# Four more stages of a decoder layer with the two parts of the activation side by side in one 512-column product

## The chip, the cores and the metric

The kernel runs on one core of one Trainium2 chip. Its engines are TensorE (PE in the profile, its weight loads PEld), VectorE (DVE), ScalarE (ACT), GpSimd (POOL) and SyncE (SP); each works through its own instructions in order. The metric is the device time of one run in microseconds, the median of the runs shown.

## The reference, cut to what matters

One layer over 256 tokens of width 1024, in float32: two self-attention mixers, cross-attention to 256 memory tokens, and a gated feed-forward block of width 2816.

```python
x = x + concat(rms(moba(h)), subln(diff(h))) @ w_out        # h = rms(x) * g, projected by w_in
h2, m = rms_norm(x, norm_g), rms_norm(mem, mem_g)
q, k, v = h2 @ wq, m @ wk, m @ wv                           # 4 heads of 256
o = softmax(q @ k.T / 16) @ v
x = x + o @ wo
h3 = rms_norm(x, ffn_norm_g)
x = x + (silu(h3 @ w_gate) * (h3 @ w_up)) @ w_down
out = rms_norm(x, final_norm_g)
```

## The kernel before

Every big product is done with numbers that are split in two: a is H + L, where H is a copy in the reduced type fp32r and L = a - H. Of the four partial products three are kept: wH aH, wH aL and wL aH. Activations lie transposed, as eight k-tiles of 128 rows by 256 tokens. Weights come in 65 chunks of 1 MB by DMA (`wr`); each chunk is split in four parts by `wpart`, ScalarE making `wh` (L124) and VectorE `wl` (L109).

A projection takes one chunk of 256 output rows: eight steps, one for each k-tile, and in a step two output halves c. There are two ways to do a step. `ws` (L302) does three products of 256 columns for each c, into one PSUM tile of 128x2x256 that holds both halves:

```python
for q, (m, b) in enumerate(((h, aH), (h, aL), (l, aH))):
    nc.tensor.matmul(o[:, c, :], m[:, k, cs], b[:, k, :], ...)
```

`ws2` (L310, L311) has H and L side by side in one tile (`hs`), and does one product of 512 columns with wh and one of 256 with wl for each c. It needs a PSUM tile of 512 columns for each half, and the two column halves have to be added afterwards: `add_halves` copies the right half to SBUF on ScalarE (L894) and adds the left one on VectorE (L896). The value weights (`as_`, L321) and the down projection have the weights as the moving side and are not touched here.

PSUM has eight tiles: three tagged `acc`, three `att` (attention logits and transposes), two `ob`. The order on every engine is the order in which the Python code writes instructions (a manual schedule). A count of steps, `state["slot"]`, rises by one in `tick()` after every step; `later(n, fn)` has `fn` written n steps ahead, and `tick` adds half a `wpart` for each step. So attention work, transposes and scalings are sprinkled between the steps of the projections by tables of step numbers.

The stages in order: q, k and v of the mixers (to about 100 us of the span); the four chunks of memory keys (`KH`, `KL`), with the end of the mixers' attention between their steps; half of the memory values; four chunks of `w_out` (evacuated by `residual`, which adds to `xT` at L746 and splits into `cH`, `cL`); four chunks of cross queries (`q_evac`); the other half of the memory values, with cross-attention (`cross_logits`, `cross_t`, `cross_pv`) between; four chunks of `w_co`; then 11 pairs of gate and up chunks and the down projection.

In the mixers, `diff_rstd` and `diff_scale` (L543 to L552) normalise the second mixer with one power on GpSimd (L265); `mix_t` (L567) transposes the result for `w_out`. In the feed-forward block the first five pairs use `ws` on the unscaled `h3`; the row factor R2 is applied in `glu` (L876 to L879, then the split at L293 and L294). Four calls of `scale_h` (L888, L287, L289) meanwhile scale `xT` by R2 and write `hs`, two k-tiles each; from pair 5 on `ws2` on `hs` is used, with `gate_evac` and `up_evac`. `x2_t` transposes `xT` back, for the end.

Of the kernel before, what the change touches and what calls it, by code (L numbers as in the profile page):

```python
# [17 lines left out]
P = 128  # L18
D = 1024
S = 256  # L20
# [17 lines left out]
def layer(ctx: ExitStack, tc: tile.TileContext, x, mem, mix_norm_g, w_in, moba_out_g, diff_lambda,  # L38
# [12 lines left out]
    def slot(i, dt=FR):  # L51
        return slots.tile([P, KT, S], dt, name=f"b{i}", tag=f"b{i}")

# [275 lines left out]
    hH, hL = slot(1), slot(2)  # L329
    h = (hH, hL)  # L330
    hF = slot(4, FT)
# [226 lines left out]
    def mix_t(e2):  # L558

        if "mix" not in M:  # L560
            M["mix"] = (slot(1), slot(2))
        mixH, mixL = M["mix"]
# [33 lines left out]
    m = (slot(4), slot(5))  # L596
# [104 lines left out]
    late = ctx.enter_context(tc.tile_pool(name="late", bufs=1))  # L701
# [3 lines left out]
    def cross_ops():  # L705
        return tuple(cx.tile([P, KT, S], FR, name="c" + n, tag="c" + n) for n in "HL")
# [15 lines left out]
    def pair(a, evac, by_k=False, late_kts=(6, 7)):  # L722

        w0, w1 = wuse(), wuse()
        o = [acc(), acc()]
        early = [k for k in range(KT) if k not in late_kts]
        if by_k:
            run([st for k in early for i, w in enumerate((w0, w1)) for st in ws_steps(o[i], w, a, [k])],
                done=False)
        else:  # L730
            for i, w in enumerate((w0, w1)):
                run(ws_steps(o[i], w, a, early), done=False)
        for i, w in enumerate((w0, w1)):
            run(ws_steps(o[i], w, a, late_kts))
# [34 lines left out]
    ev = residual(sqa, *h2, G_CROSS)  # L769
# [4 lines left out]
    q2 = (slot(1), slot(2))  # L774

    def q_evac(i, o):
        split(q2[0][:, 2 * i:2 * i + 2, :], q2[1][:, 2 * i:2 * i + 2, :], o)
# [50 lines left out]
    def cross_pv(hd):  # L828
        if not oT:
            oT.extend(cross_ops())  # L830
# [9 lines left out]
        split(oT[0][:, 2 * hd:2 * hd + 2, :], oT[1][:, 2 * hd:2 * hd + 2, :], o)  # L840
# [11 lines left out]
    h3 = (slot(1), slot(2))  # L852
    sqb = const.tile([P, 2, 256], FT, name="sqb")
    ev = residual(sqb, *h3, G_FFN)
    pair(oT, ev, True)
    for i in (2, 3):
        single(oT, ev, i)
# [4 lines left out]
    aHs = [slot(3), slot(4), slot(6)]  # L862
    aLs = [slot(5), slot(7), ff.tile([P, 6, S], FR, name="aL")]
# [7 lines left out]
    def glu(j, og, ou):  # L871
        R = R2[0].to_broadcast([P, 2, 256])
        t1 = ff.tile([P, 2, 256], FT, name="t1", tag="t1", bufs=2)
# [17 lines left out]
    def add_halves(o, tag):  # L891
        t = ff.tile([P, 2, 256], FT, name=tag, tag=tag, bufs=2)
        for c in range(2):
            nc.scalar.activation(t[:, c, :], o[c][:, 256:512], AF.Copy)  # L894
        for c in range(2):
            nc.vector.tensor_tensor(t[:, c, :], o[c][:, 0:256], t[:, c, :], op=OP.add)  # L896
        return t

    def gate_evac(j, o):
        t = add_halves(o, "t1")  # L900
# [4 lines left out]
    def up_evac(j, o, sg):  # L905
        t = add_halves(o, "ag")
        nc.vector.tensor_tensor(t, t, sg, op=OP.mult)
        split(*act(j), t)
# [122 lines left out]
```

## Time and profile before

| what | value |
|---|---|
| median of 3 runs | 429.34 us (429.2, 429.34, 432.31) |
| the profiled execution | 429.74 us |
| its span, first to last instruction | 428.0 us |
| mean granted TensorE clock over the span | 0.997 |
| busy: PE / PEld / DVE / ACT | 97% / 90% / 68% / 60% |
| steps of a `ws` chunk, of a `ws2` chunk | 8, 8 |

The profiled execution lies 0.40 us above the median of the runs, and 1.74 us above its own span. Busy time of PE counts pipelined products that overlap one another, so the pace of products is read from their starts and not from their durations.

### The profile page before, as it was taken

What the parts mean: (1) busy time and instruction counts of PE and PEld (TensorE: products, weight loads), DVE (VectorE), ACT (ScalarE), POOL (GpSimd) and SP (SyncE); (2) the same over time, 40 slices, a digit from 0 to 9 for tenths busy, and PEclk for the clock granted to TensorE, in tenths of its full rate; (3) what the DMA queues carried; (4) which work ended last, traced back from release to release, by engine and by line L of the source; (5) the groups of instructions that cost most, each with busy time, mean ns of one, the idle gap of its engine ahead of it and who ended that gap; (6) DMA issues with size and microseconds to landing.
All of it is one profiled execution on the core that took longest, in us unless ns stands there. A gap on an engine that the chain in (4) does not pass through costs nothing.

```text
span 428.0 us, 7419 instructions
## 1 busy us (share of the span) xinstructions
PE 417.0 (97%) x2900; PEld 386.7 (90%) x2900; DVE 290.1 (68%) x583; ACT 254.9 (60%) x550; POOL 27.5 (6%) x75
## 2 busy tenths in 40 slices
PE   8998999999999999999999999999999999999994
PEld 5996899979998999998999999999888888888883
DVE  2886738899497766586658678887666666744434
ACT  3778878789565663475546576565656655544313
POOL 4740200000010000000000100000000000000001
PEclk9999999999999999999999999999999999999998
DMA  8989782345438536344534846647763685555002
GB/s 252 302 229 278 198 238 81 118 125 190 179 115 289 187 100 195 101 129 158 192 114 121 269 151 188 186 124 242 248 196 102 194 296 186 208 197 196 1 2 98
DMA packets 57987, 74.62 MB, mean 174 GB/s; under 512 B 1688, under 2 KB 49596, under 8 KB 57952
## 3 DMA queue, kind: packets, MB, share of 16 engines
q1 hardware_dynamic: 56224, 69.87, 50.9%
q0 software_dynamic: 1424, 3.89, 4.1%
q8 instruction: 23, 0.38, 0.4%
q10 hardware_dynamic: 304, 0.40, 0.3%
q14 instruction: 12, 0.10, 0.1%
HBM read 72.50 MB, written 1.64 MB: 173 GB/s over the span
## 4 chain that ended last, share of the span: by engine, by line
PE 81%; DMA 6%; DVE 5%; POOL 3%; ACT 2%; issue 2%; POOLq 0%; DVEq 0%; ACTq 0%
PE acc L302 30%; PE y L321 13%; PE acc L321 9%; PE att L302 5%; PE acc L310 5%; PE att L310 5%; PE att L311 3%; PE acc L311 3%; DMA strip_d<-strip 2%; DMA bias<-strip_d 2%; DMA tT<-in_rel_bias_table_dram 2%; PE oc L838 1%; PE att L794 1%; DVE wl L109 1%; POOL strip L218 1%
## 5 line engine op out<-in xcount | busy, mean ns | idle before, releaser
L109 DVE TENSOR_TENSOR wl<-wr,wh 128x512 fp32r<-128x512 f32 x258 | 164.6, 684 | 32.4 <-ACT wh L124 32.0
L124 ACT ACTIVATE wh<-wr 128x512 fp32r<-128x512 f32 x258 | 146.0, 621 | 55.1 <-PE y L321 20.1
L302 PE MATMUL acc<-b,wh 128*128 128x256 f32 x688 | 128.2, 286 | 0.0
L302 PEld LDWEIGHTS acc<-b,wh 128*128 128x128 f32 x688 | 106.9, 191 | 0.3
L302 PE MATMUL acc<-b,wl 128*128 128x256 f32 x344 | 97.5, 283 | 0.5 <-DVE wl L109 0.5
L302 PEld LDWEIGHTS acc<-b,wl 128*128 128x128 f32 x344 | 65.8, 191 | 0.9 <-DVE wl L109 0.9
L321 PE MATMUL y<-wh,b 128*128 128x512 f32 (+1 forms) x190 | 51.8, 349 | 0.0
L321 PE MATMUL acc<-wh,b 128*128 128x512 f32 x128 | 40.6, 399 | 0.3 <-ACT wh L124 0.3
L321 PE MATMUL y<-wl,b 128*128 128x512 f32 (+1 forms) x110 | 38.1, 347 | 0.0
L321 PEld LDWEIGHTS y<-wh,b 128*128 128x128 f32 x190 | 33.6, 189 | 4.8
L310 PE MATMUL acc<-hs,wh 128*128 128x512 f32 x96 | 37.8, 393 | 0.0
L310 PE MATMUL att<-hs,wh 128*128 128x512 f32 x96 | 37.8, 393 | 0.0
L302 PE MATMUL acc<-cH,wh 128*128 128x256 f32 x128 | 36.4, 284 | 0.0
L302 PE MATMUL acc<-cH,wl 128*128 128x256 f32 x128 | 36.0, 281 | 0.0
L302 PE MATMUL acc<-cL,wh 128*128 128x256 f32 x128 | 36.0, 281 | 0.0
L311 PE MATMUL acc<-hs,wl 128*128 128x256 f32 x96 | 27.1, 283 | 0.0
L311 PE MATMUL att<-hs,wl 128*128 128x256 f32 x96 | 27.1, 283 | 0.0
L321 PE MATMUL acc<-wl,b 128*128 128x512 f32 x64 | 25.2, 394 | 1.5 <-DVE wl L109 1.5
L321 PEld LDWEIGHTS acc<-wh,b 128*128 128x128 f32 x128 | 22.5, 189 | 4.0 <-ACT wh L124 0.5
L302 PEld LDWEIGHTS acc<-cH,wh 128*128 128x128 f32 x128 | 24.1, 188 | 0.3 <-DVE b L294 0.2
L302 PEld LDWEIGHTS acc<-cL,wh 128*128 128x128 f32 x128 | 24.1, 188 | 0.0
L302 PEld LDWEIGHTS acc<-cH,wl 128*128 128x128 f32 x128 | 24.1, 188 | 0.0
(212 smaller groups left out, 631.2 us busy)
## 6 DMA issues: line engine op xcount, KB each, us to landing
wr<-in_w_gate_dram SPq DMA_DIRECT2D x11, 1024.0 KB, 5.5
wr<-in_w_up_dram SPq DMA_DIRECT2D x11, 1024.0 KB, 5.5
wr<-in_w_down_dram SPq DMA_DIRECT2D x11, 1024.0 KB, 4.9
wr<-in_w_in_dram SPq DMA_DIRECT2D x10, 1024.0 KB, 9.4
wr<-in_w_ck_dram SPq DMA_DIRECT2D x4, 1024.0 KB, 5.0
wr<-in_w_cv_dram SPq DMA_DIRECT2D x4, 1024.0 KB, 5.0
wr<-in_w_out_dram SPq DMA_DIRECT2D x4, 1024.0 KB, 5.0
wr<-in_w_cq_dram SPq DMA_DIRECT2D x4, 1024.0 KB, 5.0
```

Of the source, the lines that this page charges most:

```text
L109: eng.tensor_tensor(l, t, h, op=OP.subtract)
L124: nc.scalar.activation(h, t, AF.Copy)
L218: nc.gpsimd.tensor_copy(strip[:, lo:hi], tT[:, b:b + 1].to_broadcast([12, hi - lo]))
L302: nc.tensor.matmul(o[:, c, :], m[:, k, cs], b[:, k, :], start=first and c == 0 and q == 0, stop=last and q == 2, skip_group_check=True)
L310: nc.tensor.matmul(o[c], h[:, k, cs], flat(a[:, k]), start=first, stop=last, skip_group_check=True)
L311: nc.tensor.matmul(o[c][:, 0:256], l[:, k, cs], a[:, k, 0, :], start=False, stop=last, skip_group_check=True)
L321: nc.tensor.matmul(o, m[:, ka, ts], b[:, kw, cs], start=start and q == 0, stop=stop and q == 2, skip_group_check=True)
L794: nc.tensor.matmul(b[:, t, :], a[:, kt, t * P:(t + 1) * P], k[:, kt, :], start=n == 0, stop=n == 5)
L838: nc.tensor.matmul(o[:, dv, :], v[:, mt, cs], p_[:, mt, :], start=n == 0, stop=n == 5)
```

## The change

`ws2` is used where `ws` was for the four chunks of memory keys, four of `w_out`, four of cross queries, four of `w_co`, and for the gate and up chunks of pairs 2, 3 and 4: 22 chunks. The activations of these lie in tiles with H and L side by side (`both`, `hl`). `two()` takes one `acc` and one `att` tile for each chunk; `add_halves` evacuates keys and queries, and `residual` adds the four quarter tiles to `xT` one by one. The first pair of gate and up keeps `ws` (`pair1`), the second too. The four calls of `scale_h` move from steps 8, 22, 36 and 50 after the first pair to steps 6, 11, 16 and 21; a pair has 16 steps. `x2_t` moves from the second to fifth pair to the first 20 steps after the second. Names in the diff as in the kernel; line numbers in the changed kernel are higher by 7 to 32, and `add_halves` has moved up to L711 and L713.

```diff
+    def both(i, dt=FR):
+
+        return slots.tile([P, KT, 2, S], dt, name=f"b{i}", tag=f"b{i}")
+
+    def hl(t):
+        return t[:, :, 0, :], t[:, :, 1, :]
...
+    def ws2_steps(o, w, a, kts=range(KT)):
+        return [(ws2, (o, w, a, k, k == 0, k == KT - 1)) for k in kts]
...
+    def two():
+        return [flat(acc()), flat(att())]
+
+    def add_halves(o, t):
+
+        for c in range(2):
+            nc.scalar.activation(t[:, c, :], o[c][:, 256:512], AF.Copy)
+        for c in range(2):
+            nc.vector.tensor_tensor(t[:, c, :], o[c][:, 0:256], t[:, c, :], op=OP.add)
+        return t
+
     for c in range(4):
         w = wuse()
-        o = acc()
-        run(ws_steps(o, w, m))
-        split(KH[:, 2 * c:2 * c + 2, :], KL[:, 2 * c:2 * c + 2, :], o)
+        o = two()
+        run(ws2_steps(o, w, m2))
+        t = mx.tile([P, 4, 256], FT, name="bias", tag="bias", bufs=2)
+        split(KH[:, 2 * c:2 * c + 2, :], KL[:, 2 * c:2 * c + 2, :], add_halves(o, t[:, 0:2, :]))
...
     def single(a, evac, i):
         w = wuse()
-        o = acc()
-        run(ws_steps(o, w, a))
+        o = two()
+        run(ws2_steps(o, w, a))
         evac(i, o)
...
             xs = xT[:, 2 * i:2 * i + 2, :]
-            nc.vector.tensor_tensor(xs, o, xs, op=OP.add)
+            for c in range(2):
+                for cs in (slice(0, 256), slice(256, 512)):
+                    nc.vector.tensor_tensor(xs[:, c, :], o[c][:, cs], xs[:, c, :], op=OP.add)
             split_g(dH, dL, i, xs, gi)
...
     def q_evac(i, o):
-        split(q2[0][:, 2 * i:2 * i + 2, :], q2[1][:, 2 * i:2 * i + 2, :], o)
+        split(q2[0][:, 2 * i:2 * i + 2, :], q2[1][:, 2 * i:2 * i + 2, :], add_halves(o, halves_sum()))
...
-    pair(h3, lambda i, o: box.append(o))
+    pair1(hl(h3), lambda i, o: box.append(o))
     glu(0, *box)
     for i in range(4):
-        later(8 + 14 * i, scale_h, i)
-    for j in range(1, 5):
-        og, ou = acc(), att()
-        later(5, x2_t, j - 1)
-        for o in (og, ou):
-            w = wuse()
-            run(ws_steps(o, w, h3))
-        glu(j, og, ou)
-    for j in range(5, NFF // 2):
+        later(6 + 5 * i, scale_h, i)
+    og, ou = acc(), att()
+    for o in (og, ou):
+        w = wuse()
+        run(ws_steps(o, w, hl(h3)))
+    glu(1, og, ou)
+    for i in range(4):
+        later(8 + 4 * i, x2_t, i)
+    for j in range(2, NFF // 2):
         for side in range(2):
             w = wuse()
-            o = [flat(acc()), flat(att())]
-            run([(ws2, (o, w, hs, k, k == 0, k == KT - 1)) for k in range(KT)])
+            o = two()
+            run(ws2_steps(o, w, hs))
```

The first place is VectorE in the memory keys, from the second mixer transpose to the third: `b` at L576 is the transposed mixer result, `wl` the low part of weights, `b` at L294 the low part of the second key chunk, `rd`, `ssb`, `rbv` belong to `diff_rstd`, and the last two rows are `diff_scale`. Before:

```order
L576 SCALAR_TENSOR_TENSOR b_1423<-att,gT,b_1422 128x256 x2
L109 TENSOR_TENSOR wl<-wr,wh 128x512
L294 TENSOR_TENSOR b_1283<-acc,b_1282 128x512
L543 COPY rd<-rl 128x4 x2
L544 TENSOR_TENSOR ssb<-ssb,rd 128x8
L545 TENSOR_TENSOR ssb<-ssb,rd 128x8
L263 TENSOR_SCALAR rbv<-ssb 128x8
L109 TENSOR_TENSOR wl<-wr,wh 128x512 x3
L549 TENSOR_TENSOR rd<-rd,rb 128x8
L552 TENSOR_TENSOR b_1306<-oh,rd 128x512 x2
```

And in the changed kernel, where the tile of the sum is named `bias`:

```order
L585 SCALAR_TENSOR_TENSOR b_1403<-att,gT,b_1403 128x256 x2
L116 TENSOR_TENSOR wl<-wr,wh 128x512
L713 TENSOR_TENSOR bias<-acc,bias 128x256
L713 TENSOR_TENSOR bias<-att,bias 128x256
L301 TENSOR_TENSOR b_1281<-bias,b_1280 128x512
L552 COPY rd<-rl 128x4 x2
L553 TENSOR_TENSOR ssb<-ssb,rd 128x8
L554 TENSOR_TENSOR ssb<-ssb,rd 128x8
L270 TENSOR_SCALAR rbv<-ssb 128x8
L116 TENSOR_TENSOR wl<-wr,wh 128x512 x3
L558 TENSOR_TENSOR rd<-rd,rb 128x8
L561 TENSOR_TENSOR b_1301<-oh,rd 128x512 x2
```

Two additions stand ahead of the subtraction of the key chunk, and with it ahead of `diff_rstd` and `diff_scale`.

The second place is VectorE after the first pair of gate and up: the four rows from `sq` on belong to `glu`, and `z` and `hs` to `scale_h`. Before, from the end of the first `glu` to the second call of `scale_h`:

```order
L294 TENSOR_TENSOR b_2820<-ag,b_2817 128x512
L109 TENSOR_TENSOR wl<-wr,wh 128x512 x4
L888 TENSOR_TENSOR z<-xT,R_2950 128x512
L289 SCALAR_TENSOR_TENSOR hs<-z,gT,hs 128x256 x2
L109 TENSOR_TENSOR wl<-wr,wh 128x512 x5
L876 TENSOR_TENSOR t_3103<-acc,R_2950 128x512
L878 TENSOR_TENSOR sq<-sq,R_2950 128x512
L879 TENSOR_TENSOR ag<-att,sq 128x512
L294 TENSOR_TENSOR b_2820<-ag,b_2817 128x512
L109 TENSOR_TENSOR wl<-wr,wh 128x512 x2
L888 TENSOR_TENSOR z<-xT,R_2950 128x512
```

In the changed kernel, from the third call of `scale_h` to the fourth; between the end of the first `glu` and these rows lie three rows of `wl`, a call, two rows of `wl`, a call and three rows of `wl`:

```order
L918 TENSOR_TENSOR z<-xT,R_2766 128x512
L296 SCALAR_TENSOR_TENSOR hs<-z,gT,hs 128x256 x2
L116 TENSOR_TENSOR wl<-wr,wh 128x512
L906 TENSOR_TENSOR sum<-acc,R_2766 128x512
L908 TENSOR_TENSOR sq<-sq,R_2766 128x512
L909 TENSOR_TENSOR ag<-att,sq 128x512
L301 TENSOR_TENSOR b_2634<-ag,b_2635 128x2x256
L116 TENSOR_TENSOR wl<-wr,wh 128x512 x2
L918 TENSOR_TENSOR z<-xT,R_2766 128x512
L296 SCALAR_TENSOR_TENSOR hs<-z,gT,hs 128x256 x2
```

All four calls now stand on VectorE between the first `glu` and the evacuation of the third pair's gate, the last behind the second `glu`; the third pair's gate chunk reads `hs` from its first step.

## Rows read from the trace of the kernel before

**Rows 1.** The page, part 1: busy time of each engine.
```profile
PE 417.0 (97%) x2900; PEld 386.7 (90%) x2900; DVE 290.1 (68%) x583; ACT 254.9 (60%) x550; POOL 27.5 (6%) x75
```

**Rows 2.** TensorE waits: us in total, times, longest.
```profile
PE acc L321 <- DVE wl L109: 1.5, 1, 1.5
```

**Rows 3.** TensorE timeline: start us, us, engine line op out<-in; first product of four chunks.
```profile
139.36 0.40 PE L302 MATMUL acc<-b,wh 128*128 128x256 f32 x2
...
162.40 0.28 PE L302 MATMUL acc<-cH,wh 128*128 128x256 f32 x1
...
221.57 0.28 PE L302 MATMUL acc<-cH,wh 128*128 128x256 f32 x1
...
232.96 0.28 PE L302 MATMUL acc<-b,wh 128*128 128x256 f32 x1
```

**Rows 4.** Tile hs: duration min/median/max ns, first and last start us.
```profile
L310 PE MATMUL acc<-hs,wh x96: 387/396/400, 292.9 to 359.6; 128*128 128x512 f32 x96
```

**Rows 5.** Lines L894 and L896: duration min/median/max ns.
```profile
L894 ACT ACTIVATE t<-acc x6: 365/366/386, 298.4 to 355.4; 128x256 f32<-128x256 f32 x6
L896 DVE TENSOR_TENSOR t<-acc,t x6: 424/424/425, 298.8 to 355.8; 128x256 f32<-128x256 f32 x6
```

**Rows 6.** Timelines around the third mixer transpose: VectorE, GpSimd, TensorE.
```profile
119.67 0.69 DVE L294 TENSOR_TENSOR b<-acc,b 128x512 fp32r<-128x512 f32 x1
...
121.19 2.01 POOL L265 TENSOR_TENSOR rb<-rbv,mhalf 128x8 f32<-128x8 f32 x1 [13.74 <-DVE rbv L263]
...
123.44 1.29 DVE L552 TENSOR_TENSOR b<-oh,rd 128x512 f32<-128x512 f32 x2
...
124.45 0.88 PE L567 MATMUL att<-ident,b 128*128 128x128 f32 x4
```

**Rows 7.** Timelines in the cross-attention part: ScalarE, then TensorE.
```profile
183.11 0.56 ACT L805 ACTIVATE ec<-att,nmc,r1s 128x256 f32<-128x256 f32 x1
...
184.17 0.59 ACT L293 ACTIVATE b<-acc 128x512 fp32r<-128x512 f32 x1
...
183.52 0.60 PE L821 MATMUL att<-ident,ec 128*128 128x128 f32 x4
...
186.52 1.60 PE L794 MATMUL att<-b,b 128*128 128x256 f32 x12
```

**Rows 8.** VectorE timeline at the end of the cross output.
```profile
240.69 0.16 DVE L764 COPY tr<-att 128x2 f32<-128x2 f32 x1 [0.33 <-PE att L761]
```

**Rows 9.** VectorE timeline at the start of the gate and up products, and TensorE.
```profile
250.28 2.49 DVE L109 TENSOR_TENSOR wl<-wr,wh 128x512 fp32r<-128x512 f32 x4
252.69 0.68 DVE L888 TENSOR_TENSOR z<-xT,R 128x512 f32<-128x512 f32 x1
253.95 0.89 DVE L289 SCALAR_TENSOR_TENSOR hs<-z,gT,hs 128x256 fp32r<-128x256 f32 x2 [0.58 <-ACT hs L287]
254.75 3.09 DVE L109 TENSOR_TENSOR wl<-wr,wh 128x512 fp32r<-128x512 f32 x5
...
257.76 0.68 DVE L876 TENSOR_TENSOR t<-acc,R 128x512 f32<-128x512 f32 x1
...
261.93 1.29 DVE L109 TENSOR_TENSOR wl<-wr,wh 128x512 fp32r<-128x512 f32 x2
...
257.08 0.40 PE L302 MATMUL acc<-b,wh 128*128 128x256 f32 x2
```

**Rows 10.** TensorE timeline at the start.
```profile
1.22 2.74 PE L198 MATMUL clock<-still 128*128 128x512 bf16 x6 [1.22 <-DVE still L195]
...
5.03 2.82 PE L281 MATMUL xb<-ident,b 128*128 128x128 f32 x12 [0.87 <-DMA b<-in_x_dram]
7.65 1.06 PE L654 MATMUL clock<-still 128*128 128x512 bf16 x2
```

**Rows 11.** Windows at the end: us, then busy us per engine, PEclk, DMA.
```profile
420.00:422.00 2.00, 1.68 (x15) 1.47 (x13) 1.72 (x6) 1.05 (x4) 0.00 (x0) 1.00 0.67 233
...
424.00:426.00 2.00, 0.00 (x0) 0.00 (x0) 0.33 (x2) 0.27 (x1) 0.00 (x0) 0.86 0.55 194
```

More of the change, by code (lines that the diff above doesn't have):

```diff
@@ L328, in layer @@
     xT = const.tile([P, KT, S], FT, name="xT")
-    hH, hL = slot(1), slot(2)
-    h = (hH, hL)
-    hF = slot(4, FT)
+    h = hH, hL = hl(both(12))
+    hF = both(45, FT)[:, :, 0, :]
     xb = []
@@ L560, in mix_t @@
         if "mix" not in M:
-            M["mix"] = (slot(1), slot(2))
-        mixH, mixL = M["mix"]
+            M["mix"] = both(12)
+        mixH, mixL = hl(M["mix"])
         bank = att()
@@ L594, in mem_scale @@
         nc.vector.tensor_scalar(memv[:, t, :], memv[:, t, :], M["r"][:, t:t + 1], None, op0=OP.mult)
-    m = (slot(4), slot(5))
+    m2 = both(45)
+    m = hl(m2)
     def mem_t(j):
@@ L693, in layer, with halves_sum @@
     KH, KL = slot(0), slot(3)
+    def two():
[6 more added lines that the diff above has]
+        return t
     for c in range(4):
         w = wuse()
-        o = acc()
-        run(ws_steps(o, w, m))
-        split(KH[:, 2 * c:2 * c + 2, :], KL[:, 2 * c:2 * c + 2, :], o)
+        o = two()
+        run(ws2_steps(o, w, m2))
+        t = mx.tile([P, 4, 256], FT, name="bias", tag="bias", bufs=2)
+        split(KH[:, 2 * c:2 * c + 2, :], KL[:, 2 * c:2 * c + 2, :], add_halves(o, t[:, 0:2, :]))
     mixer.close()
     late = ctx.enter_context(tc.tile_pool(name="late", bufs=1))
+    def halves_sum():
+        return late.tile([P, 2, 256], FT, name="sum", tag="sum", bufs=2)
     cross = ExitStack()
@@ L705, in cross_ops @@
     def cross_ops():
-        return tuple(cx.tile([P, KT, S], FR, name="c" + n, tag="c" + n) for n in "HL")
+        return cx.tile([P, KT, 2, S], FR, name="cHL", tag="cHL")
     gfin = late.tile([P, D], FT, name="gfin")
@@ L724, in pair @@
         w0, w1 = wuse(), wuse()
-        o = [acc(), acc()]
+        o = [two(), two()]
         early = [k for k in range(KT) if k not in late_kts]
         if by_k:
-            run([st for k in early for i, w in enumerate((w0, w1)) for st in ws_steps(o[i], w, a, [k])],
+            run([st for k in early for i, w in enumerate((w0, w1)) for st in ws2_steps(o[i], w, a, [k])],
                 done=False)
@@ L731, in pair @@
             for i, w in enumerate((w0, w1)):
-                run(ws_steps(o[i], w, a, early), done=False)
+                run(ws2_steps(o[i], w, a, early), done=False)
         for i, w in enumerate((w0, w1)):
-            run(ws_steps(o[i], w, a, late_kts))
+            run(ws2_steps(o[i], w, a, late_kts))
             evac(i, o[i])
@@ L768, in layer @@
     sqa = const.tile([P, 2, 256], FT, name="sqa")
-    ev = residual(sqa, *h2, G_CROSS)
+    ev = residual(sqa, *hl(h2), G_CROSS)
     for i in range(4):
         single(M["mix"], ev, i)
-    q2 = (slot(1), slot(2))
+    q2 = hl(both(12))
     def q_evac(i, o):
-        split(q2[0][:, 2 * i:2 * i + 2, :], q2[1][:, 2 * i:2 * i + 2, :], o)
+        split(q2[0][:, 2 * i:2 * i + 2, :], q2[1][:, 2 * i:2 * i + 2, :], add_halves(o, halves_sum()))
     r1s = const.tile([P, 2], FT, name="r1s")
@@ L829, in cross_pv @@
         if not oT:
-            oT.extend(cross_ops())
+            oT.append(cross_ops())
         pH, pL = PS.pop(hd)
@@ L839, in cross_pv @@
                     n += 1
-        split(oT[0][:, 2 * hd:2 * hd + 2, :], oT[1][:, 2 * hd:2 * hd + 2, :], o)
+        H, L = hl(oT[0])
+        split(H[:, 2 * hd:2 * hd + 2, :], L[:, 2 * hd:2 * hd + 2, :], o)
     later(7, cross_rstd)
@@ L850, in layer @@
     mem_v(1)
-    h3 = (slot(1), slot(2))
+    h3 = both(12)
     sqb = const.tile([P, 2, 256], FT, name="sqb")
-    ev = residual(sqb, *h3, G_FFN)
-    pair(oT, ev, True)
+    ev = residual(sqb, *hl(h3), G_FFN)
+    pair(oT[0], ev, True)
     for i in (2, 3):
-        single(oT, ev, i)
+        single(oT[0], ev, i)
     cross.close()
     ff = ctx.enter_context(tc.tile_pool(name="ff", bufs=1))
-    aHs = [slot(3), slot(4), slot(6)]
-    aLs = [slot(5), slot(7), ff.tile([P, 6, S], FR, name="aL")]
+    b45 = hl(both(45))
+    aHs = [slot(3), b45[0], slot(6)]
+    aLs = [b45[1], slot(7), ff.tile([P, 6, S], FR, name="aL")]
     def act(j):
@@ L872, in glu @@
         R = R2[0].to_broadcast([P, 2, 256])
-        t1 = ff.tile([P, 2, 256], FT, name="t1", tag="t1", bufs=2)
+        t1 = halves_sum()
         sg = sq[:, j % 2 * 512:(j % 2 + 1) * 512].rearrange("p (a b) -> p a b", a=2)
@@ L889, in scale_h @@
         split_g(hs[:, :, 0, :], hs[:, :, 1, :], i, t, G_FFN)
[L891 to L897, printed above, removed]
     def gate_evac(j, o):
-        t = add_halves(o, "t1")
+        t = add_halves(o, halves_sum())
         sg = sq[:, j % 2 * 512:(j % 2 + 1) * 512].rearrange("p (a b) -> p a b", a=2)
@@ L905, in up_evac @@
     def up_evac(j, o, sg):
-        t = add_halves(o, "ag")
+        t = add_halves(o, ff.tile([P, 2, 256], FT, name="ag", tag="ag", bufs=2))
         nc.vector.tensor_tensor(t, t, sg, op=OP.mult)
@@ L929, in layer, with pair1 @@
     box = []
-    pair(h3, lambda i, o: box.append(o))
+    def pair1(a, evac):
+        w = wuse(), wuse()
+        o = [acc(), acc()]
+        for i in range(2):
+            run(ws_steps(o[i], w[i], a, range(KT - 2)), done=False)
+        for i in range(2):
+            run(ws_steps(o[i], w[i], a, range(KT - 2, KT)))
+            evac(i, o[i])
+    pair1(hl(h3), lambda i, o: box.append(o))
     glu(0, *box)
     for i in range(4):
-        later(8 + 14 * i, scale_h, i)
-    for j in range(1, 5):
-        og, ou = acc(), att()
-        later(5, x2_t, j - 1)
-        for o in (og, ou):
-            w = wuse()
-            run(ws_steps(o, w, h3))
-        glu(j, og, ou)
-    for j in range(5, NFF // 2):
+        later(6 + 5 * i, scale_h, i)
[7 more added lines that the diff above has]
+    for j in range(2, NFF // 2):
         for side in range(2):
             w = wuse()
-            o = [flat(acc()), flat(att())]
-            run([(ws2, (o, w, hs, k, k == 0, k == KT - 1)) for k in range(KT)])
+            o = two()
+            run(ws2_steps(o, w, hs))
             if side == 0:
```

## The prediction

> **What bounds the kernel now.** I read the page's busy times first, then the waits of TensorE, then its timeline at the starts of chunks, then the timelines of the other engines where the change puts work. TensorE is busy for 417.0 of 428.0 us [rows 1], and its longest wait is 1.5 us [rows 2], with five shorter ones after it. So the time is the sum of TensorE's products; work on another engine is free as long as TensorE never has to wait for it, and every wait that is added is paid in full. The reader is to look for two things: the pace of the products, taken from their starts, and how late the vector engine is at the places where TensorE will need something from it.
>
> **What the products gain.** A `w_out` chunk in the old form takes (162.40 - 139.36) / 4 = 5.760 us, a `w_co` chunk (232.96 - 221.57) / 2 = 5.695 us [rows 3]. In the new form the 96 steps on `hs` begin from 292.9 to 359.6, (359.6 - 292.9) / 95 = 0.702 us for a step of two sets, so the eight steps of a chunk take 5.617 us [rows 4]. A set, one product of 512 and one of 256 columns, takes 351 ns against 360 for three of 256: nearly the same number of columns, one start fewer. 18 chunks (keys, `w_out`, queries, six gate and up) gain 0.143 us each and four of `w_co` 0.078: 2.57 + 0.31 = **2.9 us gained**. The trace has the new form already, so this is the surest term; its bounds are 2.0 (all 22 at the small end, with some lost at chunk borders) and 3.1 (all at the large one).
> The Trainium skill (TensorE: Matmul & The Clock Gate, section Back-to-back issue gap) gives a gap of columns / 2.4 GHz + 2.5 ns, which makes 327.5 ns of the old set and 325.0 of the new one, as an estimate: 0.9 us over 352 sets in place of 2.9, and a sum that is 2.0 us higher. The rows show a larger cost of one start than the page, and I keep theirs.
>
> **What the evacuations add.** In place of one subtraction behind one copy, a key or query chunk now has two copies of 0.37 us on ScalarE and two additions of 0.42 us on VectorE [rows 5], then the old copy and subtraction. ScalarE and VectorE are busy 60% and 68% [rows 1]; their work as such fits. But the two engines take turns: the split now begins only when the additions are done. From ScalarE's first copy to the first use of the sum this is about 1.2 us (two copies of 0.37 and the last addition of 0.42). I go through the places where something is queued behind it.
>
> Keys. The second key chunk is subtracted at 119.67 [rows 6]; behind that in VectorE's order come the statistics of the second mixer, GpSimd's power of 2.01 us from 121.19, and the scaling from 123.44, which the third transpose of `mix_t` at 124.45 already waits for a little: its four products take 0.88 us, where four others take 0.60 [rows 6, 7]. With both engines busy up to there, the additions move all this by 0.75 us of additions and about 0.5 of waiting for ScalarE's copy, so the transpose ends about 1.2 us later than before, while TensorE should have been 0.5 us earlier by then. **Cost 1.7 us**, bounds 0.8 (the idle stretch of VectorE ahead absorbs part) and 2.6 (the power is started late). It is paid by TensorE, since the key products behind the transpose stand in its order.
>
> `w_out` and cross queries. `residual` has four additions of 0.42 in place of one of 512 columns (0.69 for one like it) [rows 5, 6]: about 0.6 us more in VectorE's order per chunk, with no one waiting in `w_out`. In the queries the `att` tiles are now shared: the first `cross_t` takes the tile of the second logits, which is free when their last exponential ends at 183.11 + 0.56 = 183.67 [rows 7], against its start at 183.52; the second takes the half tile of the third query chunk; the third logits need that chunk's split and the tile of the first transposes. ScalarE begins that chunk at 184.17 (it is behind with exponentials); 2 x 0.37 and 2 x 0.42, then a copy of 0.59 and a subtraction of 0.69 end at 187.0, with hand-overs 187.2, and the subtraction for the first transposes, right behind, some 0.6 later at 187.8. Before, the logits started at 186.52 [rows 5 to 7], and TensorE would be there 0.2 us earlier now. **Cost 1.5 us**, bounds 0.3 and 2.5.
>
> `w_co`. VectorE goes from one `residual` to the next without a rest; four times 0.6 us makes the copy of the row sums, at 240.69 [rows 8], some 2.2 us late; 0.33 us idle there, and the five steps of TensorE (3.6 us) that `later` sets between the row sums and the first use of the row factor, hide most. **Cost 0.4 us**, bounds 0 and 1.5.
>
> **The moved scalings.** This is the largest term. Pair 2 now needs all of `hs`, and the calls that write it stand on VectorE one behind the other, with the second `glu` and the weights' parts between. From the end of the first `glu` at 250.28 the rows give each piece [rows 9]: a `wl` 0.605 us (2.42 to the next row for four); a `scale_h` 2.06 (252.69 to 254.75, ScalarE's turn within); a `glu` 4.17 (257.76 to 261.93, two turns of ScalarE); and from the start of a `scale_h` to its first ready k-tile 1.26 (253.95 - 252.69) + half of 0.89 = 1.71. In the order of the change: 3 `wl` 1.81, scale 2.06, 2 `wl` 1.21, scale 2.06, 3 `wl` 1.81, scale 2.06, 1 `wl` 0.60, `glu` 4.17, 2 `wl` 1.21, 1.71: together 18.70, so k-tile 6 is ready at 268.98. TensorE begins the third pair at 257.08 less some 0.36 for the four transposes that no longer lie before it (0.60 us with their overlapped end [rows 7]), 256.72, and six steps of 0.702 later, at 260.93, wants that tile. It waits 1.4 us at k-tile 4 (ready at 250.28 + 8.95 + 1.71 = 260.94) and 6.6 at k-tile 6. **Cost 8.1 us**, bounds 6.0 (if the turns of ScalarE fall between other work) and 9.5. What is queued behind on VectorE, the next pair's `wl` and additions, then has 8 us of lead to give away, and I see no further wait from it. `x2_t` costs the same in its new place. No DMA is added or moved on a queue; the weight loads follow their parts.
>
> **The clock.** At the end of the run TensorE's last product ends 1.68 us into the window from 420 [rows 11], 421.7; the granted clock in the window from 424 is 0.86, so it fell from 2.4 to 1.2 GHz at about 425.4, after 3.8 us of rest. At the start it stands at the lower level: six products of 512 columns take 2.74 us where two take 1.06, so 0.42 us from start to start, and those two, at 7.65, are still as slow [rows 10]; work had begun at 1.22, and from 5.03 on it had no pause. A rest of 6.6 us in the middle is longer than the 3.8, so I take it that the clock falls there too, and comes back after at least 3.5 (5.03 to 8.5) and perhaps 7.3 us of work (from 1.22). At the lower level a set takes 640 ns (768 columns at 1.2 GHz by the rows' 0.42 for 512), 45% of that time is lost: 1.6 to 3.3 us. **Cost 2.4 us**; its lower bound is 0, since a rest between has not been seen in this trace.
>
> **Sum.** 429.74 - 2.9 + 1.7 + 1.5 + 0.4 + 8.1 + 2.4 = 440.9 us for an execution like the profiled one, which lies 0.4 above the median: 440.5.
>
> **Rivals.** First, the other side: the wait for the fourth `scale_h` does not arise, because VectorE reaches it in time. For that its 18.7 us must become 12.7, which leaves 2 us of waiting and no fall of the clock. With every turn of ScalarE gone it would be 13.5 (1.75 us in the `glu`, which is 4.17 less four pieces of 0.605, and at most 0.85 in each `scale_h`, 2.06 less two such pieces), so it must come near that, as it might if VectorE's queue were further ahead than in this trace. Then the time is 429.3 - 2.9 + 2.0 and some 1 us for the other places, 429.4, the same; with those hidden as well 426.5. Chance 6%.
> Second, the wait comes but the clock stays up: 438.1, and with the wait and the cross part at their low bounds 434.8. The order of the waits speaks for a part of it: TensorE works for 1.4 us between its two rests. Chance 16%.
> Third, PSUM: `two()` takes two tiles at a time, and a late evacuation on `att` blocks TensorE at more places than the three I found, at about 1 us for each of the eight chunks of keys and queries: 446. For it speaks that VectorE is behind from 116 to 126 us [rows 6]; against it, that the keys' half tiles come free a chunk ahead of need. Chance 9%.
> Fourth, the weight loads set the pace. The page counts PEld 90% busy [rows 1], and the change takes away 352 of them; were a load 120 ns of every set, 42 us would go: 399. The Trainium skill (Perfetto Trace Analysis, section Identifying the Most-Contended Engine) tells to judge TensorE's headroom by this busy share. Against it stand the sets on `hs`, two loads in 351 ns where three took 360 [rows 3, 4]. Chance 1%.
>
> **How the numbers follow.** The forecast with its terms near their values has 67%; 1% is left for what I don't see. All ends that make it shorter give 433.3 (429.3 - 3.1 + 0.8 + 0.3 + 6.0), all others 446.7 (429.3 - 2.0 + 2.6 + 2.5 + 1.5 + 9.5 + 3.3); the range from 434.5 to 445 holds the forecast, the second rival and part of the third. Within 1% (425.1 to 433.6), about what a measurement of this kernel can tell from no change, lies most of the first rival and a little of the second: 9%; faster, above all the fourth rival, 3%; slower 88%.
>
> **What the profile would show.** The waits of TensorE would have one new leader: `hs` from VectorE's line of `split_g`, 6 to 7 us at once in the third pair's gate chunk, near 262 to 270 us, with a granted clock below 1 in the windows right behind. `hs` products and those on the new tiles would start 230 and 120 ns apart. The third `mix_t` transpose and the third `cross_logits` would show waits of 1 to 2 us. If the new wait is shorter than 4 us, or the clock stays at 1.00, the sum is wrong by that much; if TensorE waits elsewhere for `att`, the third rival holds.

## The result and the profile after

The changed kernel takes **443.46 us** (443.1 to 443.77, 4 runs) against 430.52 us for the kernel before (429.2 to 432.31, 4 runs): a ratio of 1.0294, 95% interval 1.0254 to 1.0333, so 3% slower. The forecast was 440.5 us, in a range from 434.5 to 445. The profiled execution took 443.35 us with a span of 441.5 us.

The busy times come first (the page, part 1, and the granted clock of part 2), to be read against [rows 1].

```profile
span 441.5 us, 6788 instructions
...
PE 418.0 (95%) x2548; PEld 369.7 (84%) x2548; DVE 303.8 (69%) x629; ACT 265.0 (60%) x578; POOL 27.5 (6%) x75
...
PEclk9998999999999999999999997999999999999998
```

TensorE has 352 products fewer and is busy 1.0 us longer, in a span that is 13.5 us longer: the time went into waits and into stretches at a lower clock (the 8 in the fourth place and the 7 in the clock's row). The view of TensorE's waits (us in total, times, longest) says which waits, against [rows 2]:

```profile
PE acc L317 <- DVE hs L296: 7.8, 2, 6.4
PE acc L331 <- DVE wl L116: 2.1, 1, 2.1
PE att L576 <- DVE b L561: 1.6, 2, 1.4
...
PE att L849 <- ACT ec L833: 0.7, 1, 0.7
PE att L822 <- DVE pL L301: 0.6, 1, 0.6
```

The first is the moved scalings, the third the third mixer transpose, the last two the first transposes and the third logits of cross-attention. The second was there before, 0.6 us shorter; it lies ahead of every changed step. TensorE's timeline (start, us, operation, idle time before it) shows where each of them stands; its chunk starts answer to [rows 3], and the rows at 127.54, 186.85 and 190.95 to [rows 6, 7]:

```profile
127.54 0.30 PE L576 MATMUL att<-ident,b 128*128 128x128 f32 x1 [1.36 <-DVE b L561]
128.04 0.55 PE L576 MATMUL att<-ident,b 128*128 128x128 f32 x3 [0.21 <-DVE b L561]
...
142.58 0.39 PE L317 MATMUL acc<-b,wh 128*128 128x512 f32 x1
...
165.18 0.39 PE L317 MATMUL acc<-cHL,wh 128*128 128x512 f32 x1
...
186.85 0.55 PE L849 MATMUL att<-ident,ec 128*128 128x128 f32 x3 [0.68 <-ACT ec L833]
...
190.95 0.50 PE L822 MATMUL att<-b,b 128*128 128x256 f32 x2 [0.64 <-DVE pL L301]
...
225.87 0.40 PE L317 MATMUL acc<-cHL,wh 128*128 128x512 f32 x1
...
237.10 0.40 PE L309 MATMUL acc<-b,wh 128*128 128x256 f32 x2
...
260.79 0.39 PE L317 MATMUL acc<-hs,wh 128*128 128x512 f32 x1
...
263.46 0.28 PE L318 MATMUL att<-hs,wl 128*128 128x256 f32 x1
265.16 0.50 PE L317 MATMUL acc<-hs,wh 128*128 128x512 f32 x1 [1.42 <-DVE hs L296]
265.50 0.28 PE L318 MATMUL acc<-hs,wl 128*128 128x256 f32 x1
...
273.20 0.79 PE L317 MATMUL acc<-hs,wh 128*128 128x512 f32 x1 [6.38 <-DVE hs L296]
...
276.63 0.78 PE L317 MATMUL acc<-hs,wh 128*128 128x512 f32 x1
```

A chunk of `w_out` now takes (165.18 - 142.58) / 4 = 5.650 us against 5.760, one of `w_co` (237.10 - 225.87) / 2 = 5.615 against 5.695 [rows 3]. The gate chunk that begins at 260.79 ends at 276.63, 15.84 us where 5.62 are its products'. VectorE's timeline shows what TensorE waits for; its rows answer to [rows 6, 9]:

```profile
122.92 0.69 DVE L301 TENSOR_TENSOR b<-bias,b 128x512 fp32r<-128x512 f32 x1 [0.70 <-ACT b L300]
...
126.70 1.29 DVE L561 TENSOR_TENSOR b<-oh,rd 128x512 f32<-128x512 f32 x2
...
266.02 0.68 DVE L906 TENSOR_TENSOR sum<-acc,R 128x512 f32<-128x512 f32 x1
267.40 0.69 DVE L908 TENSOR_TENSOR sq<-sq,R 128x512 f32<-128x512 f32 x1 [0.70 <-ACT sq L907]
...
271.39 0.68 DVE L918 TENSOR_TENSOR z<-xT,R 128x512 f32<-128x512 f32 x1
272.65 0.88 DVE L296 SCALAR_TENSOR_TENSOR hs<-z,gT,hs 128x256 fp32r<-128x256 f32 x2 [0.58 <-ACT hs L294]
```

The second `glu` stands from 266.02 on where the fourth scaling is wanted, and that begins at 271.39, after the `glu` and two subtractions of weights. The clock is read from windows (bounds, length, busy us by engine, then PEclk):

```profile
38.70:42.10 3.40, 3.40 (x11) 2.72 (x10) 2.57 (x8) 2.92 (x9) 0.00 (x0) 0.50 1.06 359
...
266.50:270.80 4.30, 0.32 (x2) 0.01 (x1) 2.81 (x6) 2.30 (x4) 0.00 (x0) 1.00 0.24 81
270.80:277.60 6.80, 4.40 (x15) 3.92 (x16) 3.36 (x7) 2.01 (x5) 0.00 (x0) 0.50 0.51 154
277.60:283.00 5.40, 5.40 (x34) 4.81 (x33) 3.34 (x6) 4.28 (x10) 0.00 (x0) 1.00 0.07 14
```

It falls to 1.2 GHz during the long rest, 4 us after TensorE's last product, and is back at 277.6. And it falls once at 38.7 us, ahead of every changed line; that fall did not stand in the profile of before:

```profile
38.70:42.10 3.40, 3.40 (x20) 2.87 (x19) 2.48 (x8) 2.90 (x9) 0.00 (x0) 1.00 1.03 371
```

**The stages.** Each trace gives the starts of some chunks; from one start to the next is a stage. I count from the last of the four chunks of value weights (V), since the steps before it are the same in both kernels; M is the first memory-value chunk, Q the first query chunk, C the first `w_co` chunk, G the first gate chunk, D the first `w_down` chunk. The first rows are starts in us.

| | V | M | Q | C | G | D |
|---|---|---|---|---|---|---|
| before | 93.20 | 128.47 | 162.40 | 207.04 | 232.96 | 360.32 |
| after | 95.13 | 131.68 | 165.18 | 211.50 | 237.10 | 373.94 |

A stage's price is its length less its length before: for the keys (131.68 - 95.13) - (128.47 - 93.20) = +1.28. All the prices below are such differences, from one profile of each kernel. Kernels that have a stage alike agree in it within 0.06 us up to G, but for two rows (0.16 in the queries' stage with queries undone, 0.28 in `w_co` with the start of before filled); the gate and up stage varies more where the clock falls in it.

| kernel | keys, V to M | `w_out`, M to Q | queries, Q to C | `w_co`, C to G | gate and up, G to D | V to D |
|---|---|---|---|---|---|---|
| the change | +1.28 | -0.43 | +1.68 | -0.32 | +9.48 | +11.69 |
| gate and up undone | +1.22 | -0.42 | +1.66 | -0.32 | 0.00 | +2.14 |
| gate and up alone | -0.01 | 0.00 | 0.00 | 0.00 | +10.30 | +10.29 |
| and queries undone | +1.26 | -0.41 | +0.16 | -0.32 | 0.00 | +0.69 |
| outputs alone | +0.01 | -0.43 | -0.03 | -0.32 | 0.00 | -0.77 |
| one pair more | +1.27 | -0.39 | +1.69 | -0.32 | +1.21 | +3.46 |
| waits filled | +1.25 | -0.41 | +1.68 | -0.32 | +7.44 | +9.64 |
| scalings early | +1.24 | -0.41 | +1.67 | -0.32 | +1.99 | +4.17 |
| new form placed | -0.18 | -0.42 | +0.21 | -0.32 | -0.04 | -0.75 |
| new form placed, start filled | -0.17 | -0.42 | +0.21 | -0.32 | -0.04 | -0.74 |
| before, start filled | -0.01 | +0.01 | -0.03 | +0.28 | +0.01 | +0.26 |
| change, start filled | +1.25 | -0.41 | +1.67 | -0.32 | +9.20 | +11.39 |

### The profile page after: what moved, and what is told of

It is laid out like the page before. It is cut to its first block, busy times and chain, and to the rows that moved or that the text cites. A ratio compares the mean times of both kernels' runs of the same rounds, so it can differ in the third digit from the quotient of the medians.

```text
span 441.5 us, 6788 instructions
## 1 busy us (share of the span) xinstructions
PE 418.0 (95%) x2548; PEld 369.7 (84%) x2548; DVE 303.8 (69%) x629; ACT 265.0 (60%) x578; POOL 27.5 (6%) x75
## 4 chain that ended last, share of the span: by engine, by line
PE 72%; DVE 11%; DMA 6%; ACT 5%; POOL 3%; issue 2%; POOLq 0%; DVEq 0%; ACTq 0%
PE acc L317 13%; PE y L331 13%; PE att L317 12%; PE acc L331 9%; PE acc L318 6%; PE att L318 6%; PE acc L309 5%; DVE wl L116 3%; DMA strip_d<-strip 2%; DMA bias<-strip_d 2%; DMA tT<-in_rel_bias_table_dram 2%; PE oc L866 1%; DVE b L301 1%; POOL strip L225 1%; ACT b L300 1%
## 5 line engine op out<-in xcount | busy, mean ns | idle before, releaser
L309 PE MATMUL acc<-b,wh 128*128 128x256 f32 x336 | 63.0, 287 | 0.0
L309 PEld LDWEIGHTS acc<-b,wh 128*128 128x128 f32 x336 | 52.1, 191 | 0.2
L309 PE MATMUL acc<-b,wl 128*128 128x256 f32 x168 | 47.7, 284 | 0.5 <-DVE wl L116 0.5
L317 PEld LDWEIGHTS acc<-hs,wh 128*128 128x128 f32 x144 | 27.4, 191 | 14.4 <-DVE hs L296 8.4
L309 PEld LDWEIGHTS acc<-b,wl 128*128 128x128 f32 x168 | 32.1, 191 | 0.9 <-DVE wl L116 0.9
L317 PEld LDWEIGHTS att<-hs,wh 128*128 128x128 f32 x144 | 27.5, 191 | 6.4
L318 PEld LDWEIGHTS acc<-hs,wl 128*128 128x128 f32 x144 | 27.5, 191 | 0.0
L318 PEld LDWEIGHTS att<-hs,wl 128*128 128x128 f32 x144 | 27.5, 191 | 0.0
L317 PE MATMUL acc<-b,wh 128*128 128x512 f32 x64 | 26.3, 410 | 0.0
L317 PE MATMUL acc<-cHL,wh 128*128 128x512 f32 x64 | 25.5, 399 | 0.0
```

Of the source, the lines that this page charges most:

```text
L309: nc.tensor.matmul(o[:, c, :], m[:, k, cs], b[:, k, :], start=first and c == 0 and q == 0, stop=last and q == 2, skip_group_check=True)
L317: nc.tensor.matmul(o[c], h[:, k, cs], flat(a[:, k]), start=first, stop=last, skip_group_check=True)
L318: nc.tensor.matmul(o[c][:, 0:256], l[:, k, cs], a[:, k, 0, :], start=False, stop=last, skip_group_check=True)
```

## The experiments

My theory is the prediction's: VectorE's order, not the amount of work, sets the loss, above all by the fourth scaling behind the second `glu`. The rivals are a price in every stage (banks of PSUM, more evacuation), a VectorE that is short of time in whatever order, and a clock that has nothing to do with the rest. The kernel before ran beside each on the same chip; its runs lie between 428.69 and 434.22 us, so a median is less sharp than the table above.

**Parts undone and alone.** The first takes gate and up back:

```diff
-        later(6 + 5 * i, scale_h, i)
+        later(8 + 14 * i, scale_h, i)
...
-    for j in range(2, NFF // 2):
+    for j in range(5, NFF // 2):
```

> Gate and up as before (pairs 2 to 4 in three products a step, the four scalings 14 steps apart); keys, both outputs and queries stay in the new form. My theory (the late fourth scaling carries the loss, 8 us of wait and over 2 us of clock): about 10 us come back, 432 to 434 us, and no wait of TensorE on hs is over 0.3 us; what is left over before, some 2 us, is keys and queries. Rival (the loss is the extra evacuation of each new chunk, in every stage, and the wait on hs would only have been another one): 438 us or more.

432.65 us against 430.93, ratio 1.0054 (1.0029 to 1.0080). Of the change's 1.0294, four fifths are gone. TensorE's longest waits:

```profile
PE acc L331 <- DVE wl L116: 3.5, 1, 3.5
PE att L576 <- DVE b L561: 1.6, 2, 1.3
```

None on `hs` is left. The wait of 3.5 us is the one at the start, longer still in this profile. The reverse, gate and up alone (`ws` instead of `ws2` for keys, both outputs and queries):

> Only the gate and up part of the change; keys, both outputs and queries as before. My theory: the two waits on hs (1.4 and 6.4 us) and the lower clock behind them are there in full, since nothing in them hangs on the earlier stages: 9.0 to 10.0 us over before. Rival (VectorE comes into this stage late because of the new residual additions and queries): the wait is shorter, under 5 us, and the kernel under 435 us.

440.76 us, ratio 1.023 (1.0192 to 1.0269), 9.8 us over before. Its waits on `hs` are 7.8 us, 6.4 the longest, as in the change: they don't hang on the earlier stages, and the rival of a VectorE that comes late from them falls. By the medians that is inside the expected 9.0 to 10.0; its stage price of 10.30 is above, by the clock (last section).

With gate and up undone, queries undone too:

```diff
-    pair(h2, q_evac)
-    single(h2, q_evac, 2)
-    single(h2, q_evac, 3)
+    pair1(hl(h2), q_evac)
+    for i in (2, 3):
+        w, o = wuse(), acc()
+        run(ws_steps(o, w, hl(h2)))
+        q_evac(i, o)
```

> Gate and up as before and the queries in three products a step too; keys and both outputs stay in the new form. My theory: the queries' net price is the 1.7 us by which the landmarks between first query chunk and first output chunk moved apart (costs 2.2 us, less 0.6 us of shorter products), so this is 1.4 to 2.0 us below the kernel with gate and up as before. Rival (that 1.7 us is the clock or the start, not the queries' later copies): within 0.5 us of it.

431.84 us, ratio 1.0021 (0.9997 to 1.0045), 0.8 us in the medians, which lies between the theory and the rival; by the stages +2.14 comes to +0.69, 1.45 us, in the expected band. This profile gives the granted clock as 0.95 where the others have 1.00, yet its stages that are alike are as long (`w_out` -0.41, `w_co` -0.32, gate and up 0.00), so I read its prices like the others'. Then the keys undone too (`acc()` and `ws_steps(o, w, m)`, split at once), so that the outputs stand alone:

> Both attention outputs alone in the new form, keys, queries, gate and up as before. My theory: eight chunks save 0.143 us each, 1.1 us, and give some 0.4 us back in additions: 0.5 to 1.1 us under before; and the keys' net price, the difference to the kernel that has the keys too, is 1.0 to 1.6 us. Rival (the four additions for one hold up the banks of PSUM and cost what the products save): no faster than before.

430.83 us, ratio 0.9997 (0.9975 to 1.0019): 0.1 us under before in the medians, where 0.5 to 1.1 were expected. The stages say -0.77, which is within what the runs can't tell from nothing; that the outputs gain is shown by the profiles alone. Keys: 0.69 + 0.77 = 1.46.

**The wait on `hs`.** One pair more in three products a step ahead of the new form:

```diff
-    og, ou = acc(), att()
-    for o in (og, ou):
+    for j in (1, 2):
+        og, ou = acc(), att()
+        for o in (og, ou):
...
-    glu(1, og, ou)
+        glu(j, og, ou)
...
-    for j in range(2, NFF // 2):
+    for j in range(3, NFF // 2):
```

> The changed kernel with one pair more (the third of gate and up) in three products a step before the new form starts; the scalings are issued at the same steps as in the change. My theory (the fourth scaling stands behind one pair's evaluation on VectorE and comes 6.4 us after its step; 11 us more of TensorE's work in front cover that): no wait on hs over 0.5 us, no lower clock in this stage, 433.0 to 434.5 us, about 9.5 us under the change. Rival (VectorE is short of time throughout this stage, so that the wait moves one pair on): a wait of 4 us or more on hs or wl in the fourth pair, 438 us or more.

434.9 us, ratio 1.0079 (1.0051 to 1.0107), 0.4 above the expected band. The wait on `hs` and the lower clock behind it are gone, 8.3 us of the 9.48. But 1.57 us should have been left from V to D (2.14 less four chunks at 0.143), and 3.46 are: there is a new wait, which makes most of the 1.9 us between.

```profile
271.72 0.39 PE L309 MATMUL att<-b,wl 128*128 128x256 f32 x1 [1.12 <-DVE wl L116]
```

This is what I had not expected, a small form of the rival: the low parts of the weights come 1.1 us late from VectorE. That it is crowded by scalings 5 steps apart fits the placed kernel below, where they stand 7 apart and this wait is 0.3 us. Next, the scalings earlier with the new form where the change has it:

```diff
-        later(6 + 5 * i, scale_h, i)
+        later(4 + 4 * i, scale_h, i)
```

> The changed kernel with the scalings issued 4, 8, 12 and 16 steps after the first pair instead of 6, 11, 16 and 21: the fourth now stands ahead of the second pair's evaluation on VectorE. My theory: VectorE's 4.1 us of evaluation and one subtraction no longer stand in front of it; the last k-tile of hs is ready some 4 to 6 us sooner, the wait on it is 0.5 to 3 us, the clock stays up, and the time is 434.5 to 439 us. Rival (what stands in front of the fourth scaling is the sum of VectorE's work, in whatever order; the second pair's evaluation then comes late and the banks of PSUM are missing): under 2 us won.

434.8 us, ratio 1.008 (1.0054 to 1.0107). The same work in another order wins 7.5 us of the stage's 9.48: the long wait is 4.8 us shorter, the short one 1.2, and the clock stays up. What is left of the two waits:

```profile
263.13 0.50 PE L317 MATMUL acc<-hs,wh 128*128 128x512 f32 x1 [0.23 <-DVE hs L296]
...
266.40 0.50 PE L317 MATMUL acc<-hs,wh 128*128 128x512 f32 x1 [1.60 <-DVE hs L296]
```

VectorE's timeline there has the fourth scaling ahead of the second `glu`:

```profile
264.60 0.69 DVE L918 TENSOR_TENSOR z<-xT,R 128x512 f32<-128x512 f32 x1
...
267.26 0.68 DVE L906 TENSOR_TENSOR sum<-acc,R 128x512 f32<-128x512 f32 x1
```

Counted from G, that scaling begins 5.95 us earlier than in the change (264.60 - 236.26 against 271.39 - 237.10). By the prediction's prices 4.17 of these are the `glu`, and three subtractions of weights at 0.6, which now stand behind it too, make the rest. So it was the order of VectorE's work, the second `glu` above all, and not its sum. Last, the wait kept and filled:

```diff
-            run(ws2_steps(o, w, hs))
+            st = ws2_steps(o, w, hs)
+            if (j, side) == (2, 0):
+                clk = obank("clock")
+                for ks, n in ((slice(0, 4), 5), (slice(4, 6), 27)):
+                    run(st[ks], done=False)
+                    for _ in range(n):
+                        nc.tensor.matmul(clk, still[:, 0:P], still, start=True, stop=True)
+                st = st[6:]
+            run(st)
```

> The changed kernel with 5 and 27 empty products of 512 columns put into TensorE's two waits on hs (products of zeros into a bank that nobody reads), so that it works while it waits. My theory: the wait itself stays (the new chunk goes on at the same moment), the granted clock stays at its upper level, and the time falls by the clock's price alone, 1.5 to 2.6 us: 441 to 442 us. Rival 1 (the lower clock is not from the idle time): no change. Rival 2 (the lower clock slowed what the scaling waits for): the wait shrinks too and more than 4 us are won.

440.39 us, ratio 1.0216 (1.0172 to 1.0259), a little under the expected 441 to 442. Its timeline, and after it a window over the end of the rest:

```profile
262.69 1.25 PE L983 MATMUL clock<-still 128*128 128x512 bf16 x5
264.26 0.50 PE L317 MATMUL acc<-hs,wh 128*128 128x512 f32 x1 [0.32 <-DVE hs L296]
265.76 6.00 PE L983 MATMUL clock<-still 128*128 128x512 bf16 x27
272.31 0.51 PE L317 MATMUL acc<-hs,wh 128*128 128x512 f32 x1 [0.54 <-DVE hs L296]
...
270.00:276.70 6.70, 6.16 (x35) 4.51 (x33) 4.10 (x9) 3.13 (x8) 0.00 (x0) 1.00 0.48 157
```

The new chunk goes on at 272.31, 78.07 us after V, as in the change (273.20 - 95.13); the clock stays at 2.4 GHz, and the stage's price falls from 9.48 to 7.44. The lower clock costs 2.0 us, and it comes from the rest.

**The start.** Six empty products in the wait at the first value chunk, in the kernel before:

```diff
         for q, (m, b) in enumerate(((aH, h), (aL, h), (aH, l))):
+            if q == 2 and FILL:
+                clk = obank("clock")
+                for _ in range(FILL.pop()):
+                    nc.tensor.matmul(clk, still[:, 0:P], still, start=True, stop=True)
```

> The kernel before with six empty products of 512 columns put into TensorE's wait at the first value chunk (1.5 us of idle time before, 2.1 us in the change, where 3.4 us at the lower clock follow). My theory: the 2 us that the change loses before any changed line are this wait: a bias transfer lands at times 0.35 us later, the idle time grows past what the clock allows, and the kernel before has the same in part of its runs (429.3 and 432.0 us). With the products no run has it: all runs within 429.0 to 429.8 us, at a mean granted clock of 0.997. Rival (the two levels of before have another cause): still runs at 431.5 us and over.

430.61 us, ratio 0.9986 (0.9962 to 1.0011). Half right. Of the 28 runs of before beside it, 13 have a mean granted clock of 0.994 or less (a fall of 3.4 us takes 0.004 off the mean), with times from 430.9 to 434.22 us; of the 12 with the products one has, at 433.64. The step is all but gone, but the other eleven lie from 429.89 to 431.61 us, not below 429.8, so the median gains 0.4 us only. In the profile of this kernel the biases come later still (first use at 37.06 us, 36.57 before) and the clock stays up. In the change:

> The changed kernel with the six empty products at the first value chunk and nothing else. My theory: 2 us of the 13.5 that the two profiles differ by are not the change's but this wait's; without it the change is 11 to 12 us over the lower level of before, 441 to 441.8 us in the median. Rival (the changed kernel's own start is slower, by its tiles' new places): 443 us or more, as measured.

441.05 us (440.63 to 442.1), ratio 1.0227 (1.0191 to 1.0263), 2.4 us under the change as it was measured first. TensorE's timeline there:

```profile
36.26 1.47 PE L336 MATMUL clock<-still 128*128 128x512 bf16 x6
38.07 0.50 PE L337 MATMUL acc<-wl,b 128*128 128x512 f32 x1 [0.34 <-DVE wl L116]
```

The kernel's own price, +11.39 from V to D, is 0.3 us below the change's, by the clock in gate and up; the 2 us were the start's. They don't come with the change in every run: the kernels with one pair more and with the waits filled are the change itself up to gate and up, and only 7 of 12 and 2 of 6 of their runs have a mean granted clock of 0.994 or less.

**Placed.** The new form only where nothing waits behind its evaluation (the second key chunk, the third query chunk and the third pair go back):

```diff
+        if c == 1:
+            o = acc()
+            run(ws_steps(o, w, m))
+        else:
...
-    single(h2, q_evac, 2)
+    w, o = wuse(), acc()
+    run(ws_steps(o, w, hl(h2)))
+    q_evac(2, o)
...
-        later(6 + 5 * i, scale_h, i)
+        later(6 + 7 * i, scale_h, i)
...
-    for j in range(2, NFF // 2):
+    for j in range(3, NFF // 2):
```

> The changed kernel with the new form taken back only where something waits behind its later evaluation: the second key chunk, the third query chunk and the third pair of gate and up are products in three again, and the four scalings are issued 7 steps apart. My theory (keys cost because the second chunk's additions stand on VectorE ahead of the scaling that the third mixer transpose waits for; queries cost because the third chunk's additions stand ahead of the third logits): from the last chunk before the keys on, keys go from +1.4 to -0.4 us net and queries from +1.45 to -0.4, outputs stay at -0.8, and gate and up come to -0.6 to 0.6; together 1 to 2 us under before, 428.9 to 430 us. Rival (it is the banks of PSUM that two half tiles take, whichever chunk has them): keys and queries keep over half of their price each, and the kernel is no faster than before.

430.22 us against 431.49, ratio 0.9973 (0.9950 to 0.9997), just above the expected 428.9 to 430. One chunk of four taken back turns the keys from +1.28 to -0.18 and the queries from +1.68 to +0.21. The rival of a price for every chunk falls; the queries' expected -0.4 is not reached, since the third logits still wait a little:

```profile
PE att L309 <- DVE wl L116: 0.3, 1, 0.3
PE att L828 <- DVE pL L301: 0.2, 1, 0.2
...
PE att L576 <- DVE b L561: 0.2, 1, 0.2
```

By the stages this kernel gains 0.75 us, not the 1 to 2 expected, and `w_out` and `w_co` make 0.74 of it: keys, queries and gate and up come to nothing together. The outputs alone had -0.77.

With the start filled as well:

> The same with six empty products in the wait at the first value chunk. My theory: the runs that lose 2 us there are gone, in the median 0.4 to 1 us under the same kernel without them, and under both kernels of the case. Rival: no difference, the start was no matter of the empty products.

429.4 us, ratio 0.9959 (0.9936 to 0.9981): the lowest median of the experiments, 0.4% under before, and 0.8 us under the same without the products. Its stages cost what they cost without them (-0.74), so the 0.8 us are the start's; the outputs alone with the start filled were not run.

## Why the prediction was right, step by step

**What bounds.** Right: every wait that was added on TensorE is in the time. The prices of the five stages add up to 11.69 us, the prediction's terms to 11.2. Idle time alone understates a wait: from 263.46 to 265.50 it is 2.04 us where the usual pace makes 0.35, so that wait costs 1.69 us and not its 1.42 of idle time.

**Products.** Mis-sized: 0.143 us a chunk holds in gate and up (5.62 us each), but `w_out` gained 0.11. From the first key chunk's start to the fourth's it is 21.42 us before (100.15 to 121.57) and 21.09 after (102.10 to 123.19), 0.11 a chunk; in the queries 20.40 (162.40 to 182.80) and 20.12 (165.18 to 185.30), 0.09. `w_co` gained 0.08 as forecast. 8 x 0.11 + 4 x 0.09 + 4 x 0.08 + 6 x 0.143 is 2.4 us in place of 2.9. The gap of the Trainium skill (TensorE: Matmul & The Clock Gate, section Back-to-back issue gap) would have given an estimate of 0.9; here the measurement decides, near the rows' figure. By that gap 512 columns are 215.8 ns, also an estimate, and the trace agrees for the 27 empty bf16 products above, which start 216 ns apart. Products of 512 columns on `hs`, in fp32r, start some 231 ns apart; whether the type or the new weights before each make the 15 ns, no run separates.

**Keys.** Net +1.1 forecast (1.7 less four chunks at 0.143), +1.28 measured, on the path named: second key chunk's subtraction at 122.92, scaling at 126.70, transpose at 127.54, each 1.2 to 1.3 us later than before once the 1.93 us of V are taken off. The placed kernel shows that this one chunk carries it.

**Queries.** Net +0.9 forecast (1.5 less 0.57), +1.68 measured. The places are the ones named, the sizes are not: the third logits, put 1.5 us late, waited 0.64, and the first transposes, put 0.15 late, waited 0.68 for the exponentials of the second logits; the second transposes show no wait in the view. That the placed kernel, whose third chunk takes no `att` tile, has no wait there at all fits the shared tiles; whether the tile or the later copies carry more of it I did not separate.

**`w_co`.** 0.4 us forecast, nothing measured: -0.32 is the products' whole gain. The copy of the row sums at 246.6 is 1.8 us late (240.69 before, and 4.14 off for G; 2.2 were forecast), and stays hidden: the first two gate and up chunks take 12.17 us in both kernels.

**Scalings.** 1.4 us at k-tile 4 and 6.6 at k-tile 6 forecast; idle 1.42 and 6.38. The order of VectorE's pieces, priced row by row, was enough. That VectorE's next weights would show no further wait is true for the change, and false once the wait is taken away (1.1 us with one pair more).

**Clock.** 2.4 us forecast, 2.0 measured by filling the rest. That the clock falls in it was right; the 3.8 us of rest read at the kernel's end are no measure of when, since it fell behind 2.13 us at the start (last section).

**The median.** 440.5 forecast, 443.46 measured. The sum of the terms was right within 0.5 us, in part by luck: queries cost 0.75 us more than forecast and `w_co` 0.4 less (+0.1 forecast, -0.32 measured), while keys, `w_out` and gate and up (+9.6 forecast, +9.48 measured) were each off by under 0.2. What the sum did not have is 2 us that the change's runs lost at their start, which the prediction took as the same in both kernels. The four times of before that were known at the end, 429.2, 429.34, 431.71 and 432.31, lie two and two on either side of such a step. Of the rivals, the shorter wait, the clock that stays up and the banks at every chunk didn't occur. The third rival's 446 does not follow from its terms (eight times 1 us on 440.5 is 448.5, or 445.3 in place of the terms for keys and queries); nothing hangs on it. The 352 weight loads less came with 2.4 us of gain in all, 7 ns each, where the fourth rival had 120.

## What to carry to other kernels

Before a cheaper form of a product moves ahead, write down the order of the engine that prepares its operand and price it row by row to the moment the operand is wanted; here one evaluation standing in front of the last piece cost more than all 22 cheaper chunks gained. A form with a longer evaluation is worth having where nobody waits behind it: here the two outputs brought the whole gain, and taking the form back in one chunk of four only brought keys and queries from a loss to about nothing. When two profiles differ, line them up at the last instruction that is the same in both, and book what lies ahead of it apart.

## What was not expected of the hardware

A transfer that lands a third of a microsecond later can cost two. The relative biases' first use on VectorE waits for their DMA; the weights' subtraction that TensorE waits for stands behind it. Two rows of before, then two of the change:

```profile
36.57 0.29 DVE L467 CUSTOM_DVE_ANT_0 e<-att,bias 128x128 f32<-128x128 f32 x1 [1.48 <-DMA bias<-strip_d]
38.02 0.50 PE L321 MATMUL acc<-wl,b 128*128 128x512 f32 x1 [1.55 <-DVE wl L109]
...
36.92 0.29 DVE L476 CUSTOM_DVE_ANT_0 e<-att,bias 128x128 f32<-128x128 f32 x1 [2.05 <-DMA bias<-strip_d]
38.37 0.53 PE L331 MATMUL acc<-wl,b 128*128 128x512 f32 x1 [2.13 <-DVE wl L116]
```

The clock then stood at 1.2 GHz from 38.7 to 42.1, and V, 93.20 before, came at 95.13. Of the ten profiles without empty products there, the two with rests of 1.30 and 1.55 us show no fall behind them, the four with 2.13 to 3.48 us show one, and of the four with 1.86 to 2.01 us two do and two don't.

In the same rest on `hs` the clock fell at different times: 4.0 us after TensorE's last product in the change, some 3.3 and 2.3 us after it in the change with its start filled and in gate and up alone (worked out from the granted clock of windows of 4 us, 0.90 and 0.81 where it fell). It then stayed down for 6.8, 6.8 and 10.2 us, and the stage cost +9.48, +9.20 and +10.30. So in these three profiles the price of the same rest has a spread of about a microsecond that no line of the kernel sets.
